# Splitting the weights of one layer by DMA: a rounding load, a negation and an accumulating load

## The chip, the cores and the metric

The kernel runs on one core of a Trainium2 chip. The metric is the device time of one execution in microseconds (us), the median of several runs. A profile of one execution stands beside it; its own time and its span are given below.

## What is computed

A network of four layers works on 1040 tokens (16 learned ones ahead of a sequence of 1024) of width 1024. Layers 1 and 4 are sliding-window attention, layer 2 is an mLSTM, layer 3 is HGRN2. Each layer normalizes its input, multiplies it by a wide input matrix, mixes over the tokens, gates, multiplies by an output matrix and adds the result to its input. The second layer, cut to what matters:

```python
q, k, v, ig, fg, og, z = split(u @ w_in, (1024, 1024, 2048, 8, 8, 2048, 2048))
qk = silu(causal_conv(concat([q, k]), conv_w, conv_b))
h = mlstm_chunkwise(q, k, v, log_i, log_f)          # 8 heads, blocks of 128 tokens
h = rmsnorm(sigmoid(og) * h, h_gain)
return (h * silu(z)) @ w_out                        # [1040, 2048] @ [2048, 1024]
```

All inputs are fp32. The kernel multiplies in a rounded 32-bit form (fp32r) and keeps accuracy by splitting each operand into a high part (the value rounded) and a low part (the value less the high part): a product is three matmuls, high by high, high by low and low by high.

## The kernel before, in words

**Activations.** The normalized input lies in SBUF, transposed, as `uh` (high) and `ul` (low), 8 slices of 128 features by 1040 tokens.

**Weights.** A weight tile is 128 partitions by 1024 columns, 512 KB. It comes from HBM in two halves of 256 KB on SP's DMA queue, each into a raw tile (`raw_tile`, two buffers), and `split` (L229) makes the two parts: ScalarE copies the raw half into `wh` with rounding (L230), VectorE subtracts that from the raw half into `wl` (L231). `wh` and `wl` have three buffers each (`bufs=3`). `weights` (L233) does this for single projections, for v and for output projections; `pair` (L325) has a `pre` of its own.

**Who uses the tiles.**
- `proj` (one tile, L271) and `proj_v`/`proj_vt` (two tiles, L530 and L472) are plain products.
- `pair` (L387) multiplies two weight tiles in one go, with a scheme of seven products instead of eight for part of the work; it forms sums of the first halves of both tiles (`sh`, `sl`) and uses prepared sums of the activations (`th`, `tl`). For that, `pre` loads the first halves of both tiles into the raw tiles, splits them, forms the sums, and then loads the second halves. The second layer has 21 pairs. In an og or a z pair the first tile is used until its last products over tokens 768 to 1039 (`m0`), the second until the end (`m1`, which follows). The second tile is first used after the products of the sums, ten steps into the pair.
- `proj_out` (L569) multiplies a head's two y slices by two weight tiles: output tiles 0 to 3 use the first, 4 to 7 the second, in each of three chunks of tokens. VectorE adds each result to the residual `x` (L572).

**The second layer in order.** First come the v projection of head 0 with the gates, q and k of head 0 and q of head 1. Then, for each head: the mixer (`s1` to `s4`, blocks of 128 tokens) woven with the q/k pair and the v projection of the next head; then the og pair and the z pair. Output projections of heads 0 to 5 follow at the end of the layer's `body`; those of heads 6 and 7 are the tail that is woven with the next layer's start. Rows of `h` are parked in HBM and fetched back.

**What sets the order.** TensorE runs in the order that is written out: lists of steps `[cost, fn, pre]`. `pre` (the loading and splitting of a tile) is called some `LOOKAHEAD = 12000.0` ns of TensorE cost ahead of its step. The order on the other engines and queues is fixed at compile time by a scheduler that takes the ready instruction of the best priority, by its own idea of durations; at run time each engine goes through its list in order and waits where it must.

**GpSimd** in the second layer does little: it clears the stacked tiles of block 0 (`stacked`, L1266) and the tile `hn` (L1339), and writes 1.0 into two columns of each v tile (L1245); in `put_v` it clears v of block 0.

Of the kernel before, what the change touches and what calls it, by code (L numbers as in the profile page):

```python
# [121 lines left out]
def hybrid_kernel(ctx: ExitStack, tc: tile.TileContext, ins, out, layers=(0, 1, 2, 3)):  # L122
# [75 lines left out]
    def raw_tile():  # L198
        return wpool.tile([P, 512], F32, tag="raw", name=nm("wr"), bufs=RAWS)
# [29 lines left out]
    def split(src, h, l):  # L229
        s.copy(h, src)  # L230
        v.tensor_tensor(l, src, h.bitcast(F32), op=ALU.subtract)  # L231

    def weights(src, kind, inrow=False):  # L233
        width = src.shape[-1]
        if inrow:
            h, l = (rrow()[:, :1024] for _ in range(2))
        else:
            h = wpool.tile([P, 1024], F32R, tag="wh", name=nm("wh"), bufs=3)
            l = wpool.tile([P, 1024], F32R, tag="wl", name=nm("wl"), bufs=3)
        for z in (slice(0, width // 2), slice(width // 2, width)):  # L240
            if raws:
                raw = raws.pop(0)
                v.tensor_copy(h[:, z], raw)
                v.tensor_tensor(l[:, z], raw, h[:, z].bitcast(F32), op=ALU.subtract)
                continue
            raw = raw_tile()[:, : width // 2]
            sp.dma_start(raw, src[:, z])
            split(raw, h[:, z], l[:, z])
        c = dict(m=128, v=256, o=512, g=272)[kind]
        return tuple(z[:, :width].rearrange("p (k c) -> p k c", c=c) for z in (h, l))  # L250
# [83 lines left out]
    def pair(src0, src1, evac0, evac1, ts, scratch, follows):  # L334
# [3 lines left out]

        def pre():
            ws = [tuple(wpool.tile([P, 1024], F32R, tag=z, name=nm(z), bufs=3) for z in ("wh", "wl")) for _ in range(2)]  # L340
            raw = {}

            def part(i, half):
                z = slice(512 * half, 512 * half + 512)
                raw[i] = raw_tile()
                sp.dma_start(raw[i], (src0, src1)[i][:, z])
                split(raw[i], *(w[:, z] for w in ws[i]))

            part(0, 0)
            part(1, 0)  # L350
            a11, a12, a21, a22 = (raw[i][:, 256 * j : 256 * j + 256] for i in range(2) for j in range(2))
            f = scratch()
            q = [f[:, 256 * z : 256 * z + 256] for z in range(3)]
# [10 lines left out]
            v.tensor_tensor(q[0], a12, q[1], op=ALU.subtract)  # L364
            parts(slice(512, 768), q[2])
            parts(slice(768, 1024), q[0])
            part(0, 1)
            part(1, 1)
            st["w"] = [tuple(z.rearrange("p (k c) -> p k c", c=P) for z in w) for w in ws]
            st["s"] = [z.rearrange("p (s k c) -> p s k c", s=4, c=P) for z in (h, l)]  # L370

# [746 lines left out]
    def layer_b(i, j, fin):  # L1118
# [129 lines left out]
        def mixer(h):  # L1248
# [14 lines left out]
            def stacked(z, cols, high, low, fill):  # L1263

                st = parts(z, cols)[0]
                g.memset(st.bitcast(F32), 0.0)  # L1266
                for o in high:
                    fill(st[o : o + NMETA])
                low(st[[o for o in (0, 32, 64) if o not in high][0] :][:NMETA], st[:NMETA].bitcast(F32))
                return st  # L1270
# [53 lines left out]
            def s2(b):  # L1324
# [11 lines left out]
                v.reciprocal(den[:cn], den[:cn])  # L1336
                W["hn", b] = hn = mix.tile([P, 256], F32, tag="hn", name=nm("hn"), bufs=2)
                if b == 0:
                    g.memset(hn, 0.0)  # L1339
                s.activation(hn[:cn], num[:cn, :256], AF.Identity, scale=den[:cn])  # L1340

            def s3(b):
# [491 lines left out]
        body += weave(last + [held], flat(zg[7]))  # L1834
        return head, body, oc[5], oc[7]

    steps = []

    def ahead_of_end(first):
        k, t = len(steps), 0.0  # L1840
# [8 lines left out]
    for pos, i in enumerate(layers):  # L1849
# [30 lines left out]
        else:  # L1880
# [7 lines left out]
            for n in (2, 1):  # L1888
                t0, t1, t2 = (at(z) for z in FIRST[n - 1])
                later(seq, *sorted([(t0, norm.squares(n))] + norm.units(n, t1, t2), key=lambda e: e[0]))  # L1890
            head = [seq]
        steps += flat(head) + body
        tail, norm = (oa, ob), nxt
    first, seq = outs(tail[0] + tail[1])
# [14 lines left out]
    for n, (cost, fn, pre) in enumerate(steps):  # L1909
        while k < len(steps) and (k <= n or ahead < LOOKAHEAD):  # L1910
            if steps[k][2]:
                steps[k][2]()
            ahead += steps[k][0]
            k += 1
        if n == 0:
            load_x(2)
        fn()
        ahead -= cost
# [110 lines left out]
```

## Time and profile before

| | |
|---|---|
| median of 3 runs | 2548.94 us (2546.22 to 2549.01) |
| the profiled execution | 2548.72 us, its span 2546.8 us |
| mean granted TensorE clock | 0.998 |
| second layer, from first q columns to last of its own output projections | about 475 to 1445 us of the span |

In the profile PE is TensorE's matmuls and PEld its weight loads, DVE is VectorE, ACT is ScalarE, POOL is GpSimd, and SP issues DMAs. L230 is line 230 of the kernel before. In a window, each engine's busy time is followed by its number of instructions. In a row of groups, busy time and the mean of one stand behind the bar, then the idle time just before and what ended it. In a row of waits stand the total in us, the number of times and the longest.

DMA queues before (packets, MB, share of 16 engines' span):

```profile
q1 hardware_dynamic: 113154, 157.51, 20.7%
q10 hardware_dynamic: 288, 0.52, 0.1%
```

### The profile page before, as it was taken

How to read it: one execution, taken by the hardware profiler on the slowest of the kernel's cores; microseconds unless marked ns; L12 is line 12 of the kernel's file. 1: busy time of each engine (PE TensorE's matmuls, PEld its weight loads, DVE VectorE, ACT ScalarE, POOL GpSimd, SP SyncE). 2: the span in 40 equal slices, each digit the busy share in tenths (PEclk: the TensorE clock that was granted, in tenths of full speed). 3: DMA queues.
4: the chain of work that ended last, by engine and by line, in shares of the span. 5: the costliest groups of instructions: out<-in, count | busy, mean ns of one | idle time of the engine just before them, and what ended most of it. 6: DMA issues, size and time to landing. Idle time of an engine off the chain costs nothing. (4 is left out here: it accounts for less than half of the span.)

```text
span 2546.8 us, 55220 instructions
## 1 busy us (share of the span) xinstructions
PE 2504.8 (98%) x20152; PEld 2450.0 (96%) x20152; DVE 2156.4 (85%) x5932; ACT 1785.0 (70%) x4787; POOL 244.2 (10%) x569
## 2 busy tenths in 40 slices
PE   9999999999999999999999999999999999999999
PEld 8899999998999999999999999999999999999999
DVE  7897899978988879789787798888878988987986
ACT  8766767577777878778772258887676857867772
POOL 0321231000000000000000000100000100321320
PEclk9999999999999999999999999999999999999999
DMA  5223212212212212222242111111111013212112
GB/s 160 61 60 95 59 55 85 74 52 57 60 54 72 71 47 62 71 62 62 75 132 93 63 51 35 35 35 35 43 35 43 29 50 98 62 49 77 57 34 87
DMA packets 113713, 161.56 MB, mean 63 GB/s; under 512 B 16521, under 2 KB 65810, under 8 KB 113442
## 3 DMA queue, kind: packets, MB, share of 16 engines
q1 hardware_dynamic: 113154, 157.51, 20.7%
q8 instruction: 159, 2.61, 0.4%
q14 instruction: 112, 0.92, 0.1%
q10 hardware_dynamic: 288, 0.52, 0.1%
HBM read 132.48 MB, written 14.92 MB: 58 GB/s over the span
## 5 line engine op out<-in xcount | busy, mean ns | idle before, releaser
L271 PE MATMUL pj<-uh,wh 128*128 128x384 f32 (+2 forms) x1680 | 570.5, 340 | 1.7 <-ACT uh L230 1.2
L271 PE MATMUL pj<-ul,wh 128*128 128x384 f32 (+2 forms) x1680 | 540.2, 322 | 1.0 <-DVE ul L647 0.4
L271 PE MATMUL pj<-uh,wl 128*128 128x384 f32 (+2 forms) x1680 | 539.8, 321 | 0.0
L271 PEld LDWEIGHTS pj<-uh,wh 128*128 128x128 f32 x1680 | 317.3, 189 | 10.1 <-issue 2.6
L271 PEld LDWEIGHTS pj<-ul,wh 128*128 128x128 f32 x1680 | 317.8, 189 | 5.6 <-DVE ul L231 1.4
L271 PEld LDWEIGHTS pj<-uh,wl 128*128 128x128 f32 x1680 | 317.0, 189 | 0.6 <-DVE wl L231 0.6
L231 DVE TENSOR_TENSOR wl<-wr,wh 128x512 fp32r<-128x512 f32 (+1 forms) x336 | 232.6, 702 | 55.2 <-ACT wh L230 53.1
L572 DVE TENSOR_TENSOR x<-x,pj 128x384 f32<-128x384 f32 (+2 forms) x480 | 234.2, 508 | 33.5 <-PE pj L569 32.5
L230 ACT CAST wh<-wr 128x512 fp32r<-128x512 f32 (+1 forms) x336 | 202.6, 613 | 84.9 <-PE pj L569 24.4
L569 PE MATMUL pj<-yh,wh 128*128 128x384 f32 (+2 forms) x768 | 253.2, 330 | 7.7 <-DVE x L572 5.4
L569 PE MATMUL pj<-yl,wh 128*128 128x384 f32 (+2 forms) x768 | 245.8, 320 | 1.0 <-DVE yl L231 1.0
L387 PE MATMUL pj<-uh,wh 128*128 128x384 f32 (+1 forms) x756 | 244.5, 323 | 1.0 <-ACT t L585 0.5
L569 PE MATMUL pj<-yh,wl 128*128 128x384 f32 (+2 forms) x768 | 245.3, 319 | 0.0
L387 PE MATMUL pj<-uh,wl 128*128 128x384 f32 (+1 forms) x756 | 238.6, 316 | 0.1
L387 PE MATMUL pj<-ul,wh 128*128 128x384 f32 (+1 forms) x756 | 238.3, 315 | 0.0
L986 ACT ACTIVATE Sm<-Sm,s 128x257 f32<-128x257 f32 (+2 forms) x272 | 131.1, 483 | 91.6 <-DVE s L983 86.1
L989 POOL TENSOR_TENSOR Sm<-Sm,s 128x512 f32<-128x512 f32 (+2 forms) x136 | 137.2, 1009 | 397.6 <-DVE s L988 389.7
L230 ACT CAST yh<-r 128x384 fp32r<-128x384 f32 (+2 forms) x120 | 57.3, 479 | 157.9 <-PE pj L569 146.5
L569 PEld LDWEIGHTS pj<-yh,wh 128*128 128x128 f32 x768 | 144.3, 188 | 11.4 <-DVE x L572 7.3
L708 ACT ACTIVATE t<-t 128x384 f32<-128x384 f32 (+3 forms) x240 | 117.6, 490 | 41.3 <-DVE t L707 39.1
L569 PEld LDWEIGHTS pj<-yl,wh 128*128 128x128 f32 x768 | 144.5, 188 | 2.0 <-DVE yl L231 1.7
L530 PE MATMUL pj<-wh,uh 128*128 128x256 f32 (+1 forms) x504 | 146.0, 290 | 0.0
(383 smaller groups left out, 7186.9 us busy)
## 6 DMA issues: line engine op xcount, KB each, us to landing
wr<-in_b_win SPq DMA_DIRECT2D x124, 256.0 KB, 2.7
wr<-in_a_win SPq DMA_DIRECT2D x78, 256.0 KB, 2.6
wr<-in_c_win SPq DMA_DIRECT2D x64, 256.0 KB, 2.7
wr<-in_a_wout SPq DMA_DIRECT2D x32, 256.0 KB, 2.7
rw<-rowsd SPq DMA_DIRECT2D x64, 128.0 KB, 3.8
wr<-in_b_wout SPq DMA_DIRECT2D x32, 256.0 KB, 2.8
parked<-r SPq DMA_DIRECT2D x12, 520.0 KB, 2.6
r<-parked SPq DMA_DIRECT2D x12, 520.0 KB, 3.5
```

The lines of the kernel that those rows point to most:

```text
L230: s.copy(h, src)
L231: v.tensor_tensor(l, src, h.bitcast(F32), op=ALU.subtract)
L271: pe.matmul(acc[:, :cn], a[:, k, :], b[:, k, c0 : c0 + cn], start=(k == 0 and i == 0), stop=(k == KT - 1 and i == 2))
L387: pe.matmul(acc[key][:, :n], p, q, start=(first and z == 0 and i == 0), stop=(last and z == 1 and i == 2))
L530: pe.matmul(acc[:cn, :nc], a[:, k, c0 : c0 + cn], m[:, kk, :], start=(k == 0 and j == 0), stop=(k == KT - 1 and j == 2))
L569: pe.matmul(acc[:, :cn], a[:, k, mc], b, start=(k == 0 and i == 0), stop=(k == 1 and i == 2))
L572: v.tensor_tensor(xt(m, c0, cn), xt(m, c0, cn), acc[:, :cn], op=ALU.add)
L708: s.activation(a[:, :cn], a[:, :cn], AF.Exp)
L986: s.activation(Sm[:nq, u, : nk + 1], Sm[:nq, u, : nk + 1], AF.Exp, scale=-1.0, bias=st[:nq, u : u + 1], accum_out=den[:nq, u : u + 1])
L989: g.tensor_tensor(Sm[:nq, :, :nk], Sm[:nq, :, :nk], den[:nq].rearrange("p (u c) -> p u c", c=1).to_broadcast([nq, 2, nk]), op=ALU.mult)
```

## The change

In the second layer's `body` a weight tile is no longer split by ScalarE and VectorE from raw halves. `by_dma` loads the whole tile of 1024 columns from HBM into `wh` by a DMA of GpSimd's queue, which rounds to the type of `wh`; ScalarE writes the negative of `wh` into `wl`; a second DMA of GpSimd's queue reads the tile from HBM again and adds it into `wl`. A pair still loads its two first halves raw on SP's queue for the sums, and its two tiles by `by_dma`. The flag `far` is set for steps of the second layer's `body`; its head (v of head 0) and tail (output projections 6 and 7), and the other layers, stay as they were. The clearing of the stacked tiles and of `hn` moves from GpSimd to VectorE.

```diff
+    def by_dma(src, h, l):
+
+        g.dma_start(h, src)
+        s.activation(l, h.bitcast(F32), AF.Identity, scale=-1.0)
+        g.dma_start(l, src, accum_op=ALU.add)
+
+    far = [False]
+
     def weights(src, kind, inrow=False):
...
-        for z in (slice(0, width // 2), slice(width // 2, width)):
+        if far[0]:
+            by_dma(src, h[:, :width], l[:, :width])
+        for z in () if far[0] else (slice(0, width // 2), slice(width // 2, width)):
...
         def pre():
             ws = [tuple(wpool.tile([P, 1024], F32R, tag=z, name=nm(z), bufs=3) for z in ("wh", "wl")) for _ in range(2)]
-            raw = {}
-
-            def part(i, half):
-                z = slice(512 * half, 512 * half + 512)
-                raw[i] = raw_tile()
-                sp.dma_start(raw[i], (src0, src1)[i][:, z])
-                split(raw[i], *(w[:, z] for w in ws[i]))
-
-            part(0, 0)
-            part(1, 0)
+            raw = [raw_tile() for _ in range(2)]
+            for z, src in zip(raw, (src0, src1)):
+                sp.dma_start(z, src[:, :512])
+            by_dma(src0, *ws[0])
...
             parts(slice(768, 1024), q[0])
-            part(0, 1)
-            part(1, 1)
+            by_dma(src1, *ws[1])
...
             def stacked(z, cols, high, low, fill):
 
                 st = parts(z, cols)[0]
-                g.memset(st.bitcast(F32), 0.0)
+                v.memset(st.bitcast(F32), 0.0)
...
                 if b == 0:
-                    g.memset(hn, 0.0)
+                    v.memset(hn, 0.0)
...
-    steps = []
+    steps, by_pool = [], set()
...
+        if i % 3 == 1:
+            by_pool |= {id(z) for z in body}
         steps += flat(head) + body
...
             if steps[k][2]:
+                far[0] = id(steps[k]) in by_pool
                 steps[k][2]()
```

## The prediction

> **What bounds the kernel now.** I read the page's head first, then the windows of the second layer (475 to 1445 us, from the first columns of q to the last of its own output products), then who TensorE waits for there, then the groups of instructions that the change touches, and last the timeline around the places where a weight buffer changes hands.
>
> ```profile
> span 2546.8 us, 55220 instructions
> PE 2504.8 (98%) x20152; PEld 2450.0 (96%) x20152; DVE 2156.4 (85%) x5932; ACT 1785.0 (70%) x4787; POOL 244.2 (10%) x569
> ```
>
> TensorE leaves 42.0 us idle in the whole span. How much of it lies where the change works is in the windows (busy time of PE, PEld, DVE, ACT, POOL, then the granted clock, the DMA share and GB/s):
>
> ```profile
> core 0: us, PE busy (x) PEld busy (x) DVE busy (x) ACT busy (x) POOL busy (x), PEclk, DMA share, GB/s
> 540.00:600.00 60.00, 57.13 (x404) 55.25 (x403) 48.95 (x151) 43.69 (x127) 0.81 (x7) 1.00 0.16 39
> 600.00:700.00 100.00, 96.15 (x613) 93.41 (x612) 91.84 (x254) 77.08 (x200) 1.62 (x10) 0.98 0.23 64
> 700.00:1100.00 400.00, 399.67 (x2744) 397.81 (x2743) 343.50 (x966) 307.10 (x796) 7.47 (x56) 1.00 0.22 64
> 1330.00:1445.00 115.00, 115.00 (x732) 115.00 (x731) 83.05 (x171) 28.10 (x56) 0.00 (x0) 1.00 0.25 79
> sum 970.00, PE 961.22 PEld 950.72 DVE 817.93 ACT 677.42 POOL 14.36; mean PE 120.15 PEld 118.84 DVE 102.24 ACT 84.68 POOL 1.79
> ```
>
> Over the 970 us PE is busy for 961.2: only 8.8 us are idle, 6.7 of them between 540 and 700, where VectorE is at its fullest (91.84 of 100 us). From 700 to 1100, and in the output projections from 1330 on, PE never stops, though VectorE is at 86% and 72%. So work taken from VectorE can give back at most 8.8 us here, and nothing in the stages that are full already. Who ended PE's waits in the same stretch:
>
> ```profile
> PE pj L387 <- DVE kwl L1316: 1.7, 2, 1.5
> PE pj L569 <- DVE x L572: 1.1, 1, 1.1
> PE pa L1410 <- ACT yh L230: 1.1, 1, 1.1
> ```
>
> These are single waits: for a low part in the mixer, for an accumulator's release, for the high part of a sum of squares. None is for a weight: that a weight comes in time costs nothing today. The question is whether that stays so.
>
> **What is removed.** The splits of the weights in the second layer, by shape:
>
> ```profile
> L231 DVE TENSOR_TENSOR wl<-wr,wh 128x512 fp32r<-128x512 f32 x148 | 100.0, 687 | 34.9 <-ACT wh L230 33.9
> L230 ACT CAST wh<-wr 128x512 fp32r<-128x512 f32 x148 | 89.6, 615 | 42.9 <-DMA wr<-in_b_win 23.8 <-PE pj L569 11.0 <-DMA wr<-in_b_wout 3.3
> L1245 POOL MEMSET v<- 128x2 f32 x57 | 4.8, 100 | 405.0 <-DVE Vl L231 324.4 <-ACT t L1216 38.0 <-ACT v L445 23.7
> ```
>
> 148 halves are 74 tiles of 128x1024: 42 in the 21 pairs, 20 in the single and v projections, 12 in six output projections. VectorE loses 100.0 us. It gains 32 memsets that GpSimd had (four in each of eight heads):
>
> ```profile
> L1266 POOL MEMSET Vh<- x8: 317/320/323, 419.3 to 1219.7; 128x258 f32 x8
> L1266 POOL MEMSET Wh<- x8: 205/205/208, 419.6 to 1218.8; 128x128 f32 x8
> L1266 POOL MEMSET kwh<- x8: 205/205/208, 419.7 to 1210.1; 128x128 f32 x8
> L1339 POOL MEMSET hn<- x8: 312/312/317, 419.9 to 1229.8; 128x256 f32 x8
> ```
>
> At GpSimd's own durations that is 8 x 1.04 = 8.3 us; VectorE ends 92 us lighter. I do not know its own price, but between 0 and twice this it is under 17 us against 100. ScalarE changes little: two casts back to back took 1.14 us (the 1351.70 row below), and one negation of 1024 columns covers the same columns, so 74 x 1.14 = 84 us come for 89.6 that go. SP's queue loses 106 of its 148 weight loads (the pairs keep 42 first halves for their sums). I take 2 us of the 8.8 us of idle time as given back: the lighter VectorE shortens the chains in the 540 to 700 stretch, but the waits named there are waits for one product after another, not for a full queue. The ends are 0 and 8.8.
>
> **What is added: a chain behind the release of a buffer.** Today a half waits in a raw tile, already loaded, for its wh/wl buffer; once the buffer is free, a cast and a subtraction finish it. After the change the first load itself writes wh, so it cannot begin before the buffer is free, and behind it stand the negation and a second load that adds into wl. Three wh/wl buffers rotate and a pair or an output projection holds two, so the second tile of the next one always takes the buffer that the first tile of the current one frees. How long PE leaves for that is read at three places. Output projection, ScalarE, then TensorE:
>
> ```profile
> 1351.70 1.14 ACT L230 CAST wh<-wr 128x512 fp32r<-128x512 f32 x2 [2.20 <-PE pj L569]
> ```
> ```profile
> 1354.43 0.34 PE L569 MATMUL pj<-yh,wh 128*128 128x400 f32 x1
> 1359.16 0.34 PE L569 MATMUL pj<-yh,wl 128*128 128x400 f32 x1
> ```
>
> At 1351.70 the buffer is released (the cast waited for PE L569). The next projection begins at 1354.43; its first four output tiles are 24 matmuls on the first weight tile, then two on the second's wh, and at 1359.16 the first on its wl. That leaves 7.5 us. The same for a v projection followed by an og pair, and for an og pair followed by a z pair (release, first use of wl in the tail of a pair):
>
> ```profile
> 818.94 1.14 ACT L230 CAST wh<-wr 128x512 fp32r<-128x512 f32 x2
> 840.42 0.62 ACT L230 CAST wh<-wr 128x512 fp32r<-128x512 f32 x1
> ```
> ```profile
> 832.42 0.34 PE L387 MATMUL pj<-uh,wl 128*128 128x384 f32 x1
> 854.95 0.34 PE L387 MATMUL pj<-uh,wl 128*128 128x384 f32 x1
> ```
>
> 13.5 us and 14.5 us. Each kind occurs five times (output projections 0 to 5; v before og in heads 1 to 5; og before z in heads 0 to 4). Elsewhere the mixer is woven in and the room is longer.
>
> The length of the chain is not in the trace, since GpSimd issues no DMA there. The nearest rows (size, median time from issue to landing), and what SP's issue takes (least, median, most, ns):
>
> ```profile
> wr<-in_b_win SPq DMA_DIRECT2D x124, 256.0 KB, 2.7
> r<-parked SPq DMA_DIRECT2D x12, 520.0 KB, 3.5
> x<-away SPq DMA_DIRECT2D x8, 128.0 KB, 4.9
> L346 SPq DMA_DIRECT2D wr<-in_b_win x84: 327/328/1455, 539.4 to 1283.6; - x84
> ```
>
> A tile is 512 KB. First load: at least 3.5 us (520 KB); at most 4.9, the small loads' time when many stand in line. I take 4.9, as 3.5 plus a slow issue like SP's slowest (1.4), because a queue written by software will hardly be quicker than SP's. Negation: 1.14, and 0.2 until ScalarE comes to it. Second load: it brings the same 512 KB and must also read what it adds to. From 256 to 520 KB costs 0.8 us, so 512 KB more are some 1.6: 4.9 + 1.6 = 6.5; its ends are 3.5 (the add is free) and 9.8 (twice the crowded load). The chain is 4.9 + 1.3 + 6.5 = 12.7 us, with ends 8.1 and 15.8.
>
> The Trainium skill ("DMA: Bandwidth & Descriptors", Anatomy of one DMA) fits a GpSimd-issued DMA by 2.0 us plus bytes over 436 GB/s, 3.2 us for a tile as an estimate; SP's 520 KB above took 3.5. With it twice the chain would be 7.5 us and the whole cost nil; the page "Collectives: The Full Stack" (The bandwidth ceiling, in Part 3) says that an add in the DMA takes two source reads, which would make it 8.7. No run here shows either yet.
>
> **The sum.** Output projections: 5 x (12.7 - 7.5) = 26 us of PE idle. V before og and og before z: 12.7 is under 13.5 and 14.5, nothing. Less 2 us given back: +24. The profiled execution took 2548.7 us, 1.9 beside its span of 2546.8; its sum is 2546.8 + 24 + 1.9 = 2572.7, and the median of the three runs is 0.2 above it, so 2573. With the chain at 8.1 the loss is 3 us; at 15.8 it is 5 x (8.3 + 2.3 + 1.3) = 60.
>
> **What else queues.** On GpSimd the second load waits for the negation, and behind it stand the next tile's first load and the v tiles' small memsets (57 of 100 ns). Those already wait up to a head's length for their buffer, and the last columns that they write are read a head later, so their delay is covered; only the clearing of a head's block 0 is followed at once, by ScalarE's copy of v. On ScalarE the negation waits for the first load, and all that stands behind it waits too: the evacuations, the exponentials of the mixer, the high parts. If ScalarE gets there in time this costs nothing; that is the third rival.
>
> **Rivals.** First, *quick loads*: both loads land like the 520 KB row. The chain is 8.1 us, the five handovers cost 3, and 2 to 5 of the idle time come back: 2547 to 2550, no change. For it: bandwidth is there, the DMA share is 0.22 to 0.25; the change adds 148 x 0.52 = 78 MB and takes away 106 x 0.26 = 28. Against: two transfers, one of them an add, must each be as fast as SP's plain ones. The Trainium skill's fit would make this the outcome.
>
> Second, *the other side*: the chain stays under 7.5 us, so no handover stalls, and the 92 us taken from VectorE close the idle time between 540 and 700, 6.7 us: 2548.9 - 6.7 = 2542. It decides from 7.5 us on down, which is under the sum of the nearest rows; against it also that PE is idle there behind single products and casts.
>
> Third, *ScalarE stands still*: the order of its instructions is fixed beforehand; where the first load lands later than that order assumes, ScalarE waits at the negation. It has 400 - 307.1 = 93 us free in 700 to 1100, in which some 31 tiles fall, 3.0 us per tile. A wait for a raw tile is already there:
>
> ```profile
> ACT wh L230 <- DMA wr<-in_b_win: 23.8, 27, 2.6
> ```
>
> 0.9 us on the mean, over 27 of the 124 loads. Under 3 us per tile it is hidden; at 4 us the 62 tiles ahead of the output projections cost 1 us each, 62 in all, and with the 24 the run takes 2635; from there the handovers at 13.5 and 14.5 go too.
>
> That the path is not taken at all I give nothing: the flag is set from the identity of the body's own steps.
>
> **How the numbers follow.** About 0.2% (5 us) is what a measurement of this kernel can tell from no change. The forecast, stalls in the output projections, has 0.60; quick loads 0.17; the other side 0.08; ScalarE standing still 0.15. Slower is the first and the last, 0.75; same 0.17; faster 0.08. The likeliest case alone runs from 2554 (a chain of 9) to 2607 (15.8). The range goes from 2546, which takes in the quick loads, to 2640, which takes in most of the third rival; left out are the other side and the worst of ScalarE.
>
> **What would show it.** In the changed kernel PE should wait for DMA at L569's counterpart five times, some 5 us each, about 22.8 + 5 us apart, and PE's share in 1330 to 1470 should fall to some 82%, with little new idle time between 700 and 1100. The landing times of GpSimd's two loads give the chain's terms at once. Wrong it would be if no such wait appears (chain under 7.5 us), if PE's idle time lies in the pairs instead (chain far over 14, or ScalarE waiting at the negation for over 3 us per tile), or if the 540 to 700 stretch fills up and nothing is lost.

## The result and the profile after

| | before | after |
|---|---|---|
| median | 2548.76 us (2546.22 to 2549.01, 4 runs) | 2611.21 us (2608.01 to 2614.18, 4 runs) |
| profiled execution, its span | 2548.72 us, 2546.8 us | 2608.01 us, 2606.2 us |
| granted TensorE clock | 0.998 | 0.987 |

The change is 62.5 us slower, a ratio of 1.0248 (95% interval 1.0236 to 1.0261). The forecast was slower by 24. In the kernel after, `split` and `by_dma` stand at L229 to L237 (first load L235, negation L236, second load L237), and `proj_out` multiplies at L572, `proj` at L281, `proj_v` at L475 and L533, `pair` at L390 (its function begins at L334 of the kernel before).

The head of the page after:

```profile
span 2606.2 us, 55129 instructions
PE 2521.6 (97%) x20152; PEld 2465.2 (95%) x20152; DVE 2079.1 (80%) x5816; ACT 1772.9 (68%) x4713; POOL 344.2 (13%) x685
```

VectorE is 77.3 us lighter and TensorE idle twice as long: 2606.2 - 2521.6 = 84.6 us, 42.0 before. TensorE also has 16.8 us more of busy time for the same 20152 matmuls. The two, 42.6 and 16.8, are the 59.4 us by which the span is longer. (The profiled execution after is the shortest of its four, so some 3 of the 62.5 us stand in no profile.) Where, by windows (columns as in the prediction's):

```profile
475.00:540.00 65.00, 54.30 (x377) 52.11 (x375) 51.17 (x115) 37.16 (x94) 6.10 (x19) 0.92 0.41 111
540.00:600.00 60.00, 56.51 (x400) 55.97 (x399) 36.00 (x108) 40.38 (x107) 7.46 (x16) 0.97 0.42 87
600.00:700.00 100.00, 93.37 (x591) 91.15 (x590) 84.52 (x246) 75.48 (x194) 9.53 (x16) 0.97 0.47 109
700.00:1100.00 400.00, 398.95 (x2733) 396.55 (x2732) 306.49 (x908) 297.85 (x759) 48.00 (x102) 1.00 0.51 117
1100.00:1250.00 150.00, 140.47 (x964) 138.43 (x964) 109.10 (x344) 102.90 (x277) 15.37 (x38) 0.98 0.48 104
1250.00:1375.00 125.00, 124.76 (x827) 123.94 (x826) 93.35 (x260) 92.76 (x228) 15.06 (x24) 1.00 0.60 155
1375.00:1520.00 145.00, 126.36 (x735) 124.53 (x734) 73.71 (x155) 26.29 (x43) 13.27 (x19) 0.92 0.40 95
```

From 700 to 1100 PE is as full as before (398.95 of 400) though VectorE went from 343.50 to 306.49 and the DMA share from 0.22 to 0.51. The loss is in three stretches: the start of the layer, around 1230, and the output projections. In all three the granted clock falls too. Whom PE waited for (rows that are much the same before are left out):

```profile
PE pj L572 <- DMA wl<-in_b_wout: 18.6, 5, 4.7
PE pj L281 <- DMA wl<-in_b_win: 7.1, 1, 7.1
PE pj L475 <- DMA wl<-in_b_win: 6.3, 1, 6.3
PE pm L1294 <- DVE r L1233: 3.5, 1, 3.5
PE pt L1368 <- ACT hn L1343: 3.5, 1, 3.5
PE pj L281 <- DMA wh<-in_b_win: 2.4, 1, 2.4
```

Before, one wait in the layer was for a weight, 0.3 us. Now eight are, 34.4 us in all: five at the output projections, as forecast, and three that were not.

**One handover.** An output projection: GpSimd's issues, ScalarE's negation, then TensorE.

```profile
1382.74 0.55 POOL L235 DMA_DIRECT2D wh<-in_b_wout  x1 [14.01 <-PE pj L572]
1386.26 1.06 ACT L236 ACTIVATE wl<-wh 128x1024 fp32r<-128x1024 f32 x1 [0.40 <-DMA wh<-in_b_wout]
1387.73 0.89 POOL L237 DMA_DIRECT2D wl<-in_b_wout  x1 [1.58 <-PE pj L572]
```
```profile
1385.15 0.34 PE L572 MATMUL pj<-yh,wh 128*128 128x400 f32 x1
1393.09 0.60 PE L572 MATMUL pj<-yh,wl 128*128 128x400 f32 x1 [3.05 <-DMA wl<-in_b_wout]
1393.48 0.54 PE L572 MATMUL pj<-yh,wh 128*128 128x400 f32 x1
1396.75 0.34 PE L572 MATMUL pj<-yl,wh 128*128 128x400 f32 x1
```

The buffer is free at 1382.74 and TensorE goes on at 1393.09: a chain of 10.3 us, in which the wait covers 3.05. In the fourth of the five the chain is 11.9 us (1465.42 to 1477.36) and the wait 4.65; in the fifth they are 12.0 us (1495.20 to 1507.23) and 4.73. Then comes what the sum did not have: behind the wait the matmuls take 0.54 us and start 0.33 apart, where 0.34 and 0.18 are usual, until 1396.75. That is half clock for some 3.4 us (the granted clock from 1393.2 to 1396.6 is 0.50), and costs some 1.7 more. The Trainium skill ("TensorE: Matmul & The Clock Gate", Part 1 and HAM oscillation) tells of half rate after an idle window of about 3.4 us, until a busy one of that length has passed, and warns of gaps above it; here the length agrees, but the wait of 3.05 us is shorter than its limit.

**The handovers that were missed.** The start of the layer, where the tile of q of head 0 wants a buffer that v of head 0 holds until its last matmul (`pj L533`):

```profile
507.55 0.73 POOL L235 DMA_DIRECT2D wh<-in_b_win  x1 [7.62 <-PE pj L533]
511.53 0.42 PE L281 MATMUL pj<-uh,wh 128*128 128x400 f32 x1 [2.44 <-DMA wh<-in_b_win]
511.54 1.05 ACT L236 ACTIVATE wl<-wh 128x1024 fp32r<-128x1024 f32 x1
512.89 0.90 POOL L237 DMA_DIRECT2D wl<-in_b_win  x1 [2.97 <-ACT wl L236]
519.25 0.70 PE L281 MATMUL pj<-uh,wl 128*128 128x400 f32 x1 [7.12 <-DMA wl<-in_b_win]
```

There is no other work in between, so nearly the whole chain of 11.7 us lies open. The other is v of head 7, whose buffer the z pair of head 5 frees at 1217.64. (Into the mixer of head 6 the code lays the single q of head 7, the z pair of head 5 and v of head 7; the order told ahead of the prediction leaves this z pair behind its own head's mixer.) In the order of time:

```profile
1217.64 0.56 POOL L235 DMA_DIRECT2D wh<-in_b_win  x1 [14.68 <-PE pj L390]
1221.84 1.06 ACT L236 ACTIVATE wl<-wh 128x1024 fp32r<-128x1024 f32 x1 [0.70 <-DMA wh<-in_b_win]
1223.31 0.91 POOL L237 DMA_DIRECT2D wl<-in_b_win  x1 [2.17 <-ACT E L1300]
1229.78 0.70 PE L475 MATMUL pj<-uh,wl 128*128 128x400 f32 x1 [6.29 <-DMA wl<-in_b_win]
```

TensorE was there after 5.9 us; the chain took 12.1.

**The whole difference, place by place.** Both kernels have the same matmuls in the same order, so the n-th matmul of one can be laid beside the n-th of the other. How much later it starts after the change, at a few places:

| start before, us | start after, us | later by, us | what lies between this row and the one above |
|---|---|---|---|
| 505.85 | 508.81 | 3.0 | layer 1, and the turn to layer 2 |
| 529.96 | 544.30 | 14.3 | q of head 0: wh and wl late, half clock |
| 545.10 | 563.71 | 18.6 | a wait through ScalarE and VectorE, half clock |
| 1199.04 | 1222.77 | 23.7 | the mixers of heads 0 to 6 |
| 1201.05 | 1232.57 | 31.5 | v of head 7 |
| 1354.43 | 1385.15 | 30.7 | head 7 |
| 1470.01 | 1529.92 | 59.9 | the output projections |
| end | | 59.4 | |

So of 59.4 us the output projections cost 29.2, the start of the layer 11.3, v of head 7 7.8, the place at 545 4.3, and some 7 are spread (5.1 of them in the mixers, 3.0 ahead of the layer's first products, and head 7 gives 0.8 back).

### The profile page after: what moved, and what is told of

It reads as the page before. It is cut to its first block, busy times and chain, and to the rows that moved or that the text cites. A ratio compares the mean times of both kernels' runs of the same rounds, so it can differ in the third digit from the quotient of the medians.

```text
span 2606.2 us, 55129 instructions
## 1 busy us (share of the span) xinstructions
PE 2521.6 (97%) x20152; PEld 2465.2 (95%) x20152; DVE 2079.1 (80%) x5816; ACT 1772.9 (68%) x4713; POOL 344.2 (13%) x685
## 3 DMA queue, kind: packets, MB, share of 16 engines
q0 software_dynamic: 21312, 77.60, 13.7%
## 4 chain that ended last, share of the span: by engine, by line
PE 48%; issue 17%; DVE 16%; ACT 10%; DMA 7%; POOL 2%; SPq 0%; DVEq 0%; POOLq 0%; ACTq 0%
PE pj L281 14%; PE pj L572 10%; PE pj L533 6%; PE pj L390 4%; PE pj L475 3%; DMA rw<-rowsd 2%; DMA wh<-in_b_win 2%; PE po L1025 1%; PE pt L1007 1%; DVE Sm L986 1%; DVE wl L231 1%; ACT Sm L989 1%; PE po L1277 1%; POOL wl L237 1%; DVE x L575 1%
## 5 line engine op out<-in xcount | busy, mean ns | idle before, releaser
L281 PE MATMUL pj<-uh,wh 128*128 128x384 f32 (+2 forms) x1680 | 571.2, 340 | 4.8 <-DMA wh<-in_b_win 2.4
L281 PE MATMUL pj<-uh,wl 128*128 128x384 f32 (+2 forms) x1680 | 540.9, 322 | 7.1 <-DMA wl<-in_b_win 7.1
L281 PE MATMUL pj<-ul,wh 128*128 128x384 f32 (+2 forms) x1680 | 541.0, 322 | 1.5 <-DVE ul L650 1.0
L281 PEld LDWEIGHTS pj<-uh,wh 128*128 128x128 f32 x1680 | 318.3, 189 | 13.2 <-issue 5.2
L281 PEld LDWEIGHTS pj<-uh,wl 128*128 128x128 f32 x1680 | 317.9, 189 | 7.5 <-DMA wl<-in_b_win 7.5
L281 PEld LDWEIGHTS pj<-ul,wh 128*128 128x128 f32 x1680 | 318.7, 190 | 6.1 <-DVE ul L650 1.6
L572 PE MATMUL pj<-yh,wl 128*128 128x384 f32 (+2 forms) x768 | 250.7, 326 | 18.6 <-DMA wl<-in_b_wout 18.6
L572 PE MATMUL pj<-yh,wh 128*128 128x384 f32 (+2 forms) x768 | 257.6, 335 | 7.5 <-DVE x L575 5.4
L572 PE MATMUL pj<-yl,wh 128*128 128x384 f32 (+2 forms) x768 | 249.9, 325 | 2.2 <-DVE yl L231 2.2
L390 PE MATMUL pj<-uh,wh 128*128 128x384 f32 (+1 forms) x756 | 245.2, 324 | 2.0 <-DVE kwl L1319 1.1
L390 PE MATMUL pj<-uh,wl 128*128 128x384 f32 (+1 forms) x756 | 239.2, 316 | 0.0
L390 PE MATMUL pj<-ul,wh 128*128 128x384 f32 (+1 forms) x756 | 239.1, 316 | 0.0
L572 PEld LDWEIGHTS pj<-yh,wl 128*128 128x128 f32 x768 | 148.2, 193 | 20.4 <-DMA wl<-in_b_wout 20.3
L572 PEld LDWEIGHTS pj<-yh,wh 128*128 128x128 f32 x768 | 147.9, 193 | 11.5 <-DVE x L575 7.3
L572 PEld LDWEIGHTS pj<-yl,wh 128*128 128x128 f32 x768 | 147.8, 192 | 3.1 <-DVE yl L231 2.8
L231 DVE TENSOR_TENSOR wl<-wr,wh 128x512 fp32r<-128x512 f32 (+2 forms) x188 | 132.5, 713 | 20.1 <-ACT wh L230 18.7
L533 PE MATMUL pj<-wh,uh 128*128 128x256 f32 (+1 forms) x504 | 146.0, 290 | 0.0
```

The costliest lines, as they stand in the source:

```text
L281: pe.matmul(acc[:, :cn], a[:, k, :], b[:, k, c0 : c0 + cn], start=(k == 0 and i == 0), stop=(k == KT - 1 and i == 2))
L390: pe.matmul(acc[key][:, :n], p, q, start=(first and z == 0 and i == 0), stop=(last and z == 1 and i == 2))
L533: pe.matmul(acc[:cn, :nc], a[:, k, c0 : c0 + cn], m[:, kk, :], start=(k == 0 and j == 0), stop=(k == KT - 1 and j == 2))
L572: pe.matmul(acc[:, :cn], a[:, k, mc], b, start=(k == 0 and i == 0), stop=(k == 1 and i == 2))
```

## The experiments

Theory: weights come late because the first load can only start into a free buffer, the chain of load, negation and second load (10 to 12 us) is longer than the room at seven handovers (two of the eight waits are for the same tile), and each stall brings half clock. Rivals: ScalarE standing at the negation; the added traffic, 78 MB; the changed orders of ScalarE and VectorE, or the clearings moved to VectorE. In what follows "late" tiles are those of output projections 1 to 5, the single tiles at the layer's start (q and k of head 0, q of head 1), and v of head 7: 15 tiles.

**Only the output projections by DMA** (`e1_oc_only`; `ocs` are their steps, projections 0 to 5).

```diff
-            by_pool |= {id(z) for z in body}
+            by_pool |= ocs
```


> Only the twelve tiles of output projections 0 to 5 take the new way; all others are split as before (the clearing stays on VectorE). Late buffers (theory): the five handovers in the output projections cost what the shift of TensorE's instructions showed there, 28.8 us, stall and half clock together: 2548.8 + 29 = 2578 us (2574 to 2581). Traffic and queue (rival: each tile that takes the new way costs its share, 62.5 us over 74 tiles, 0.84 us each): 12 x 0.84 = 10, 2559 us.

Measured: 2582.58 us, before 2547.16, ratio 1.0140 (1.0125 to 1.0155). In its profile the first three of the five waits were 3.0 to 3.3 us long, and the end came 29.1 us later than before: the whole loss of this stage with 12 of 74 tiles. By the medians it is 35.4 us, a little more than expected; the profiled execution is the shortest of the four. Either is far from the 10 us of a share for each tile.

**All tiles but the late ones** (`e2_not_late`, 59 tiles).

```diff
-            by_pool |= {id(z) for z in body}
+            by_pool |= {id(z) for z in body} - late
```


> All tiles take the new way but those whose buffer is freed late: output projections 1 to 5, the three single projections at the layer's start, and v of head 7 (15 of 74 tiles, split as before). Late buffers: 2611.2 less 28.8 (output projections), 11.2 (start) and 7.8 (v of head 7) = 2563 us, and no wait of TensorE for a weight's DMA is left. Traffic and queue: 59 tiles x 0.84 = 50, 2598 us. What is left over 2549 is what neither explains yet: waits of ScalarE at the negation and slower loads of rows.

Measured: 2560.25 us, ratio 1.0059 (1.0043 to 1.0076). One wait of PE for a weight is left, 0.3 us long: 51 of the 62 us are these 15 tiles. Some 10 to 13 stay (10.4 by the spans, 13.1 by the medians).

**The clearings alone** (`e3_memsets`, an edit of the kernel before).

```diff
-                g.memset(st.bitcast(F32), 0.0)
+                v.memset(st.bitcast(F32), 0.0)
...
-                    g.memset(hn, 0.0)
+                    v.memset(hn, 0.0)
```

> The kernel before with only the 32 clearings moved from GpSimd to VectorE. Late buffers and traffic alike: no change, 2549 us within 2. If the clearings on VectorE are a cost of the change: up to 8 us, 2557.

Measured: 2551.54 us, ratio 1.0016 (1.0006 to 1.0025); its span is 0.3 us longer than before. By the times they cost some 4 us (1.5 to 6.4), by the spans almost nothing; the profiled execution is the shortest of its ten (2548.90), so the two do not contradict each other. On VectorE the 32 clearings take 7.0 us. At one place the profile shows them: TensorE's wait at the turn to layer 2 (440.80) is 1.87 us long, 0.68 before. In every run with the clearings on VectorE it is 1.84 to 1.88. What it costs is won back later in this profile.

**Buffers that come free earlier** (`e6_spare`: after, with the second tile of output projections 1, 3 and 5 in two buffers of q, idle by then, so that every `wh`/`wl` comes free one projection earlier).

```diff
+        if spare is not None:
+            h, l = (spare()[:, :1024] for _ in range(2))
...
-                          fin if h == 7 else None, h == 6) for h in range(8)}
+                          fin if h == 7 else None, h == 6, spare if h in (1, 3, 5) else None) for h in range(8)}
```


> The changed kernel, with the second weight tile of output projections 1, 3 and 5 in two buffers that lie idle by then (those of q, of the mixer), so that each tile's buffer there is free a whole projection (some 22 us) ahead; DMAs, negations and their number as in the change. Late buffers: the five waits at the output projections go, 28.8 us: 2611.2 - 29 = 2582 us (2576 to 2586). Traffic and queue: nothing of the traffic changes, 2611 us.

Measured: 2584.01 us, ratio 1.0144 (1.0130 to 1.0158), 27 under the change. In its profile the matmul that starts at 1354.43 before comes 33.3 us later, that of 1470.01 33.9: the output projections cost 0.6 us with the same DMAs, the same negations and the same traffic.

**TensorE kept busy in the wait** (`e5_fill`: after, with 17 matmuls whose result nobody reads, ahead of the second tile of projections 1 to 5).

```diff
+                if fill and (n, m, k) == (0, 4, 0):
+                    idle = psa()
+                    for z in range(FILL):
+                        pe.matmul(idle[:, :384], uh[:, 0, :P], uh[:, 0, :384], start=True, stop=True)
```

> The changed kernel with 17 idle matmuls (128x384, about 3.0 us, results unused) written ahead of the first product on the second weight tile in output projections 1 to 5, where TensorE stands 3.0 to 4.7 us. If the half clock after a stall comes from standing still (theory): the stall is filled, the clock stays at 1.0 there, and only the five gaps of 18.6 us remain of the 28.8: 2611.2 - 10 = 2601 us. If the clock falls for another reason (rival): 2611 us, or more by what the idle matmuls run over.

Measured: 2603.55 us, ratio 1.0221 (1.0204 to 1.0238), 7.7 under the change, though it has 85 matmuls more. The window from 1400 to 1425, first of the change, then of this one:

```profile
1400.00:1425.00 25.00, 21.81 (x131) 21.45 (x130) 12.20 (x26) 4.16 (x7) 2.90 (x4) 0.93 0.53 127
```
```profile
1400.00:1425.00 25.00, 24.60 (x156) 24.26 (x154) 14.10 (x30) 4.90 (x8) 2.90 (x4) 1.00 0.43 111
```

The granted clock is 1.00, not 0.93: the half clock comes from standing still, and is a term of its own beside the wait. Matmul by matmul the stage costs 21.0 us here, 29.2 in the change; the whole span is no shorter in this profile (2606.1 us, the longest of the four), since other places lost as much. At the fifth projection the 17 matmuls leave a wait of 2.20 us (to 1504.43), and the clock is at half again from 1504.7 to 1508.

**The chain cut in halves** (`e7_halves`: each of the three steps in two pieces of 512 columns).

```diff
-        g.dma_start(h, src)
+        for z in zs:
+            g.dma_start(h[:, z], src[:, z])
...
```

> The changed kernel with each of the three steps of a tile in two halves of 512 columns: two loads, two negations, two adding loads. If bytes and the negation make up much of the chain of 10.3 to 11.9 us, it shortens by about 1.5 us (256 KB instead of 512 ahead of the first negation 0.8, half a negation 0.5, less what the second adding load queues): 7 handovers x 1.5 = 10 us less, 2601. If the fixed part of a DMA and the issue on GpSimd (0.55 and 0.89 us each in the changed kernel) make it up, twice as many issues lengthen it: 2611 to 2620 us.

Measured: 2604.95 us, ratio 1.0220 (1.0206 to 1.0233). The halves landed 4.1 and 4.9 us after issue, against 3.8 and 5.5 for whole tiles: in twos, a load of half the size is hardly quicker. (These are the input matrix's tiles; for the output projections it is 3.2 and 4.7, against 3.7 and 5.4.) Matmul by matmul the handovers did get cheaper, 24.1 us at the output projections, 8.5 at the start of the layer and 4.0 at v of head 7, 36.6 in all against 48.3; most of that was lost again elsewhere, and 6 us are left by the medians. PE's waits for wl at the output projections went from 18.6 to 13.4 us. ScalarE's waits at the negation of the input matrix's tiles rose from 33.1 to 54.9 us, and a wait of TensorE through VectorE at the start of the layer from 3.5 to 6.1.

**Every tile with room** (`e9_mixer0`: as `e2_not_late`, with the second head's v and the k pair, which are laid into head 0's mixer, split as before as well; `e10_room`: the same, but all 12 tiles of the output projections by DMA, with the buffers of `e6_spare`).

```diff
-        late.update(id(z) for z in flat(qg[0]) + flat(kg[0]) + flat(qg[1]) + flat(vg[7]))
+        late.update(id(z) for z in flat(qg[0]) + flat(kg[0]) + flat(qg[1]) + flat(vg[1]) + kk + flat(vg[7]))
```

> The tiles that come with room went by DMA in an earlier run and 10.3 us were left, most of it between 540 and 625 us, in the mixer of head 0, where the negation on ScalarE stood 2.9 us for its first load and TensorE then 3.5 us for ScalarE, with half clock behind it. Here the tiles that are laid into that mixer (the second head's v and the pair of k) are split as before as well; those of heads 1 to 6 still go by DMA. Theory (a wait of ScalarE in a place where TensorE hangs on ScalarE): 2551 to 2554 us, the waits of TensorE at 560 and 624 us gone, while ScalarE still waits for the first load in heads 1 to 6. Rival (the added traffic, or ScalarE's waits wherever they are): the 10 us stay, 2557 to 2560 us.

> As the run that leaves the starts of the layer, head 0's mixer and the last v as before, but all twelve tiles of the output projections go by DMA, the second tile of projections 1, 3 and 5 in buffers of q that are idle by then, so that every buffer comes free one projection earlier. Theory (a load that starts into a free buffer in time costs nothing): within 3 us of that run, 2551 to 2556 us. Rival (the output projections cost something beside the late buffers): 2560 us or more. If the 100 us taken from VectorE were worth anything, this one would be under 2549.

Measured: 2559.80 us, ratio 1.0039 (1.0027 to 1.0052), and 2560.47 us, ratio 1.0045 (1.0031 to 1.0059); before 2549.22. The first is a miss. Of the two waits that it was to remove, the one at 560 us went (0.6 us is left) and the one at 624 stayed (4.2 us to 622.90, ScalarE having stood 3.1 us at a negation). But the 10 us did not sit there: the matmuls that run from 545 to 662 us in the kernel before take 1.3 us less in this run. The second confirms the theory again: the output projections add 0.7 us. It also answers the change's own question: with VectorE 68 us lighter the kernel is 11 us slower, not faster, though TensorE waits for a weight only once, for the second tile of v of head 2:

```profile
692.33 0.45 PE L491 MATMUL pj<-uh,wl 128*128 128x400 f32 x1 [1.42 <-DMA wl<-in_b_win]
```

**Negation on GpSimd** (`e8_pool_neg`: `e2_not_late`, with GpSimd doing the negation).

```diff
-        s.activation(l, h.bitcast(F32), AF.Identity, scale=-1.0)
+        g.tensor_scalar(l, h.bitcast(F32), -1.0, None, op0=ALU.mult)
```


> As e2_not_late (late-freed tiles split as before), but the negation is done by GpSimd, not by ScalarE; ScalarE then never stands at a load. ScalarE waits (theory for what e2 left): the gaps of TensorE behind them go, 2560 - 8 = 2552 us (2549 to 2555). Traffic: 2560 us as e2, the loads being the same. If GpSimd's negation disturbs VectorE or is far slower than ScalarE's 1.06 us: above 2560.

Measured: 2592.75 us, ratio 1.0174 (1.0160 to 1.0189). The negation takes 2.84 us there, 1.06 on ScalarE, and TensorE loses in the mixers (window 700 to 1100 of `e2_not_late`, then of this):

```profile
700.00:1100.00 400.00, 399.06 (x2736) 396.47 (x2736) 305.32 (x905) 295.37 (x757) 46.35 (x93) 1.00 0.51 118
```
```profile
700.00:1100.00 400.00, 385.54 (x2596) 379.98 (x2595) 309.64 (x850) 256.03 (x683) 123.95 (x118) 0.99 0.47 108
```

It cannot tell what ScalarE's standing costs, since the step that replaces it has its own price.

**The last 10 us.** Five tries, and none of them settled it. First, added traffic with all splits as before (`e4_traffic`: 148 loads of 512 KB from HBM to HBM on GpSimd's queue).

```diff
+        for d in dump:
+            g.dma_start(d[:, : src.shape[-1]], src)
```

> All tiles are split as in the kernel before; beside that GpSimd's queue issues for each of the 74 tiles two loads of 512 KB that nobody reads (HBM to HBM, so the bytes are those of the change, the path not quite), and the clearing stays on VectorE. It asks what the 11 to 13 us are that were left with the late buffers taken out. ScalarE waits (theory: the negation stands at the head of ScalarE's list until the first load lands): none of that is here, 2549 to 2553 us. Traffic (rival: the row loads of the mixer land later beside the added bytes): 2558 to 2562 us.

Measured: 2667.06 us, ratio 1.0463 (1.0449 to 1.0478), a miss as a test: with no buffer to wait for, the loads ran ahead into layer 1, where GpSimd has work of its own, and TensorE waited 53.5 us for that (`PE pt L1019 <- POOL Sm L1004`; 7.6 us in the kernel before). All of the loss lies ahead of layer 2 (its first matmuls start 111 us late). What it shows is the price of loads on the queue of an engine that others wait for.

Second, rows. In `e10_room` VectorE waited 49.9 us for the mixer's row loads between 650 and 1245, 13.7 before. So these loads were asked for earlier, in `s3` behind the update of C and no more in `s1` (`e11_rows_early`), or on ScalarE's queue (`e14_rows_act`), each beside the kernel before with the same edit.

```diff
-                if b + 1 < NB:
-                    fetch(b + 1)
...
+                if b + 3 < NB:
+                    fetch(b + 3)
```
```diff
-                sp.dma_start(z[:, :, :cn], R["rows_d"][:, h, c0 : c0 + cn].partition_broadcast(P))
+                s.dma_start(z[:, :, :cn], R["rows_d"][:, h, c0 : c0 + cn].partition_broadcast(P))
```


> As the run with room for every tile (2560.5 us), and the row loads of the mixer are asked for right after the update of C that frees their buffer, some 3 us earlier than at the start of the next block. Between 650 and 1245 us VectorE waited 49.9 us in 27 places for these loads there, 13.7 us in 11 places in the kernel before; they landed 4.1 us after issue, 3.8 before. Theory (the weight tiles' traffic makes the row loads late, VectorE hangs on them, and TensorE on VectorE): the waits for rows go below 20 us and the time falls to 2550 to 2554. Rival (the rows are hidden, the 10 us are the orders of ScalarE, with the negation among them, and VectorE): 2558 to 2562 though the waits for rows are shorter.

> The kernel before with the row loads asked for earlier in the same way, as the measure for the other run. Theory: in it the waits for rows (13.7 us) cost nothing that TensorE sees, 2547 to 2551 us. If it is faster than 2545, the gain of the other run would not be the traffic's alone.

> Writing wh and wl out added 129 to 136 GB/s of traffic and left the row loads at 3.8 us and VectorE's waits for them at 12.5 us, so traffic does not make the rows late. In the run with room for every tile, SP's queue shows a row load right behind a pair's raw load that had stood for VectorE's sums (699.35 and 701.79 us, VectorE then waiting at 705.63). Theory: the row loads stand behind the pairs' raw loads in SP's queue, and VectorE, from which they wait for the raw buffers, waits for the rows. Here, in the kernel with room for every tile (2560.5 us), ScalarE's queue issues the row loads, so that they stand behind no raw load: VectorE's waits for rows between 650 and 1245 us fall from 49.9 to under 20 us and the time to 2550 to 2555 us. Rival (the 10 us are the orders of ScalarE and VectorE, the row waits only VectorE arriving earlier): 2557 to 2562 us.

> The kernel before with the row loads issued on ScalarE's queue, as the measure for the other run. Theory: its row waits cost nothing that TensorE sees, so 2546 to 2551 us; a gain beyond that would not be the change's.

| | time, us | ratio to before | VectorE's row waits, 650 to 1245 |
|---|---|---|---|
| rows earlier, with the change | 2557.28 | 1.0038 (1.0024 to 1.0052) | 47.9 us |
| rows earlier, kernel before | 2545.82 | 0.9996 (0.9987 to 1.0005) | 12.9 us |
| rows by ScalarE, with the change | 2554.68 | 1.0041 (1.0027 to 1.0054) | 46.2 us |
| rows by ScalarE, kernel before | 2542.52 | 0.9988 (0.9979 to 0.9996) | 13.6 us |

(The kernel before took 2547.31 us beside the first two and 2545.91 beside the last two, so that the 2554.68, though inside the range that the theory gave, is no gain.) The 10 us stay in both, and so do the waits, which neither edit shortened. That these waits are what TensorE feels is thereby not shown; a VectorE with less to do also comes to the same loads earlier and waits longer. At one place it can be followed: in the change's own profile VectorE waits 3.94 us for a row load, until 602.90, and TensorE then 1.17 and 1.15 us for VectorE (to 603.70 and 605.29), some 3 us with the half clock behind it. (The row loads on ScalarE's queue make the kernel before 0.1% faster, the only edit here that beats it.)

Third, traffic in the right places (`e13_writes`: splits as before, and GpSimd's queue writes `wh` and `wl` of the tiles of `e9_mixer0`, 55 with the two of output projection 0, to an unused tensor).

```diff
+        for z in (h, l):
+            d = dump.pop(0)
+            dump.append(d)
+            g.dma_start(d[:, : z.shape[-1]], z.bitcast(F32))
```

> Every weight split as before (clearings on VectorE, as in the change), and for the 53 tiles that go by DMA in the run with head 0's mixer as before, GpSimd's queue also writes wh and wl, once split, into an unused tensor: two transfers of 512 KB for a tile, in the same places as the two loads of the change, with nobody waiting for them but the buffer's next user. It adds the traffic and leaves ScalarE's and VectorE's orders as they were. Theory (the traffic makes the row loads late and costs the 8 to 10 us that were left): 2556 to 2560 us, VectorE's waits for the rows between 650 and 1245 us at 40 us or more, 13.7 before. Rival (the changed orders of ScalarE and VectorE cost them, traffic does not): 2548 to 2553 us.

Measured: 2586.94 us, ratio 1.0153 (1.0139 to 1.0167), more than either side expected. The row loads did not become late by it (3.8 us to landing, and VectorE's waits):

```profile
DVE E L1312 <- DMA rw<-rowsd: 12.5, 10, 2.6
PE po L1346 <- DVE t L1229: 11.3, 5, 3.3
```

So 129 to 136 GB/s of traffic in all (62 to 67 before, 111 to 117 in `e10_room`) leave the rows alone. The loss came elsewhere: SP's raw loads landed after 3.6 us, 2.7 before, and TensorE waited some 2 to 3 us once a head where it had hardly waited. Whether that is the traffic or the buffers, which the writes hold longer, this run does not part.

Fourth, ScalarE. In `e16_hold` the negation and the second load are written 3.5 us of TensorE's work later than in `e10_room`.

```diff
+        def low():
+            s.activation(l, h.bitcast(F32), AF.Identity, scale=-1.0)
+            g.dma_start(l, src, accum_op=ALU.add)
+
         g.dma_start(h, src)
-        s.activation(l, h.bitcast(F32), AF.Identity, scale=-1.0)
-        g.dma_start(l, src, accum_op=ALU.add)
+        held.append((spent[0] + HOLD, low))
```

> As the run with room for every tile (2560.5 us); the negation and the second load of a tile are placed 3.5 us of TensorE's work later in the order of the engines, so that the first load has landed when ScalarE comes to the negation. In that run ScalarE waited 23.9 us in 20 places between 650 and 1245 us for first loads. Theory (ScalarE standing at the negation holds up what is queued behind it, and that is the 10 us): those waits fall under 8 us and the time to 2549 to 2554. Rival (the 10 us do not come from these waits, but from the other changes of order and load): the waits fall and the time stays at 2556 to 2561 us.

Measured: 2556.47 us, ratio 1.0030 (1.0021 to 1.0040), in the interval of the others. ScalarE's waits for first loads stayed, 24.2 us; 23.9 in `e10_room`. The order on ScalarE is made by a scheduler by its own durations, and a later place in the program apparently did not move it; the wait could not be taken away in this manner. In this run and in `e11_rows_early` PE waits for no weight in the layer, so the 8 to 10 us are there without a single late tile.

What stays open, then, is the 8 to 11 us of a change in which weights are late by 1.4 us at most. Their place is known, by laying matmul beside matmul: the stretch from 662 to 1172 us of the kernel before, the mixers of heads 1 to 6, takes 8.9 us longer in `e10_room` and 9.0 in `e9_mixer0` (5.6 to 6.5 in the last three runs with the change, 0.3 in `e3_memsets`). Of the 8.9, 5.2 are idle time of TensorE, in waits of 1.4 us and less with several causes; the rest is busy time, and no half clock falls in the stretch. Their cause is not: rows' issue and queue are out as far as these edits reach, and head 0's mixer is out. The clearings may hold 1.5 to 6 of the 8 to 11 us by the times, though their one profile is only 0.3 us longer. ScalarE's and VectorE's orders and the traffic of an adding load remain.

## Why the prediction was right and wrong

- **Work taken from VectorE is worth nothing here: right.** It lost 77.3 us of busy time (92 were forecast), and with room for nearly every tile (`e10_room`) the kernel is still 11 us slower. Whether the 2 us that the sum took came back is not shown: the stretch from 545 to 662 us is 2.8 us shorter in `e10_room`, but it is also 4.6 and 3.1 us shorter in `e12_before_rows` and `e15_before_act`, where VectorE has all its work.
- **The chain: right in its sum, with terms that were each too long.** Forecast 4.9 + 1.3 + 6.5 = 12.7 us, measured 10.3 to 12.0 at the output projections. (The ends given for it, 8.1 and 15.8, and the 7.5 hold 1.1 us for the negation, where the sum has 1.3.) The terms, from the table of DMA issues and the groups of ScalarE (475 to 1500 us):

```profile
wh<-in_b_win POOLq DMA_DIRECT2D x62, 512.0 KB, 3.8
wl<-in_b_win POOLq DMA_DIRECT2D x62, 512.0 KB, 5.5
rw<-rowsd SPq DMA_DIRECT2D x64, 128.0 KB, 5.1
L236 ACT ACTIVATE wl<-wh 128x1024 fp32r<-128x1024 f32 x73 | 77.2, 1057 | 45.3 <-DMA wh<-in_b_win 33.1 <-DMA wh<-in_b_wout 12.0
```

  The first load took 3.8 us, close to SP's 520 KB row (3.5), and the add 1.7 more. The Trainium skill's fit ("DMA: Bandwidth & Descriptors", Anatomy of one DMA) gave 3.2 for both as an estimate: 0.6 short for the load and 2.3 for the add. For the two source reads of an add (the Trainium skill, "Collectives: The Full Stack", The bandwidth ceiling, in Part 3) the prediction reckoned 1.2 us more; the add took 1.7 more than the load, 1.45 times as long.
- **The output projections: right in place and number, and near in size by luck.** Five stalls, 26 us forecast, 29.2 measured. Its working was 5 x 5.2 us of idle time; the idle time is 18.6 and the rest, 10.6, is half clock. The sum put this term at nothing without a reason: it priced a stall at its idle time alone. `e1_oc_only` gives this term by itself, `e6_spare` takes it away, `e5_fill` parts the two.
- **The step that failed: "Elsewhere the mixer is woven in and the room is longer."** It was put down without a row, and two handovers had less room than the 7.5 us of the output projections. At the start of the layer no mixer is woven in: the single tiles follow each other and all buffers are held by v, 11.3 us. At v of head 7, behind the last pair in the mixers, the mixer is woven in, but only five of its matmuls fall between release and first use, 7.8 us. With the 29.2 they are 48.3 of the 59.4 us, and `e2_not_late` shows them gone together. A list of every release and first use, where I took three kinds, would have shown the 5.9 us of room at 1223.
- **V before og and og before z, 13.5 and 14.5 us: right.** From 700 to 1100 PE has 1.05 us of idle time, 0.33 before, and none of PE's waits for a weight is at `pair` (L390).
- **ScalarE standing still (third rival): at two places.** The first load issued at 545.71 landed 8.9 us later, while SP moved row loads of the first mixer, and ScalarE stood:

```profile
554.67 1.06 ACT L236 ACTIVATE wl<-wh 128x1024 fp32r<-128x1024 f32 x1 [3.88 <-DMA wh<-in_b_win]
557.56 0.62 DVE L1227 SCALAR_TENSOR_TENSOR r<-t,bcols,r 128x384 f32<-128x384 f32 x1 [5.68 <-ACT r L1225]
560.38 0.24 PE L1294 MATMUL pm<-q,r 128*16 128x16 f32 x2 [3.49 <-DVE r L1233]
```

  ScalarE to VectorE to TensorE, and half clock behind it: 4.3 us. The second place is the start of the mixer of head 1:

```profile
631.84 1.06 ACT L236 ACTIVATE wl<-wh 128x1024 fp32r<-128x1024 f32 x1 [2.84 <-DMA wh<-in_b_win]
638.96 0.69 PE L1368 MATMUL pt<-ident,hn 128*128 128x128 f32 x2 [3.45 <-ACT hn L1343]
```

  VectorE waited 3.15 us for ScalarE in between, and half clock follows here too; but the kernel before has waits and half clock of its own at these matmuls, and over the stretch from 545 to 662 us the change loses nothing against it. Over the layer ScalarE's idle time at the weights hardly rose, 45.3 us at the negation, 42.9 at the casts before. The rival's threshold, 3.0 us a tile, was not reached: the mean wait was 0.6 us (45.3 over 73 negations).
- **Quick loads and the other side** are out: the chain is above 7.5 us at each of the five.

## What to carry to other kernels

When a load writes straight into a buffer that TensorE reads, its time moves from before the release to behind it: list every release and the first use after it, the first and last of a stage above all, and hold the chain against the shortest, not the usual, room. Price a stall of TensorE with the clock behind it; here that added more than half of the wait again. And where TensorE is as full as here, work taken from another engine has little to set against such a chain.

## What the runs showed of the hardware that had not been expected

- A wait of TensorE of some 3 us (3.05 at 1393.09) was followed by some 3.4 us at half clock; TensorE kept busy on unused data through the same wait kept the clock at 1.00 (1400 to 1425 us of `e5_fill`), and a wait of 2.20 us at its fifth projection was again followed by 3.4 us at half clock.
- A rounding load of 512 KB of the input matrix on GpSimd's queue landed 3.8 us after issue, an adding one 5.5; halves of 256 KB took 4.1 and 4.9, when sent in twos.
- GpSimd's own time for an issue was 0.55 us for the first and 0.89 us for the adding load.
- A negation of 128x1024 took GpSimd 2.84 us and ScalarE 1.06.
